# Five Strassen units instead of four in two output projections, woven in an order written out by hand

## The chip, the cores and the metric

The kernel runs on one core of a Trainium2 chip. The metric is the device time of one execution in microseconds (us); lower is better. TensorE is PE in the profile (its weight loads PEld), VectorE is DVE, ScalarE is ACT, GpSimd is POOL and SyncE is SP.

## The reference

The whole kernel computes two residual layers on 512 tokens of width 1024: a dilated attention mixer and an mLSTM mixer, each followed by a gated FFN of width 2816, and a last RMS norm. The change concerns only the second matrix product of the two FFNs, and the norm that follows the second:

```python
def swiglu(xn, w_in, w_out):
    gu = xn @ w_in
    return (jax.nn.silu(gu[..., :D_FF]) * gu[..., D_FF:]) @ w_out      # [512, 2816] @ [2816, 1024]

for i in range(2):
    ...
    h = h + swiglu(rms_norm(h, ffn_norm[i]), ffn_w_in[i], ffn_w_out[i])
return rms_norm(h, final_norm)
```

All of it is float32.

## The kernel before

**Split products.** Each float32 operand is split into a high part in TensorE's fp32r format and a low part, the difference. One product is made of three matmuls: high by high, high by low, low by high (`SPLITS`). Splitting a chunk of weights costs an ACT copy (`whi`, line 209) and a DVE subtract (`wlo`, line 210) of 128x1024 elements; splitting an operand of hidden rows costs an ACT copy (line 1114) and a DVE subtract (line 1108) of 128x512.

**The output projection.** The 2816 rows of `w_out` are eleven pairs of row tiles (a pair is 2 x 128 rows), the 1024 columns two halves, and the 512 tokens two halves. `output_products` (line 1090) does part of this by the Strassen-Winograd scheme of two by two by two blocks: a unit takes two row pairs, both column halves and both token halves, and does seven products P1, P2, P5, P6, P7, P3 and P4 in place of eight. The operands of these are sums and differences of weights and of hidden rows. `UNITS = 4` units cover eight row pairs; the three other pairs (`REST`) are done plainly, once for each column half, and are called plain or rest items. In layer 0 a product is 24 matmuls of 256 columns, a rest item 24 of 512 (`tile_mm`, line 1289, matmul at line 1292); in layer 1 a product is 12 matmuls of 512 columns, a rest item 24 (`multiply_half`, matmul at line 1674).

**Sums of weights.** In layer 1 each unit keeps a running sum `t` of weight chunks (tile f1T, 128x1024), which passes through P1, P5, P6 and P4: after P1 and after P5 it is negated on ACT (line 1163), and a DMA issued by POOL adds other weight rows from DRAM to it (`add_rows`, line 1160); after P6 it is negated again. P7 loads another chunk, to which DVE adds `t` (line 1182; line 1177 in layer 0), and then a DMA adds rows to `t` for P4. P2, P3, P7 and the rest items load raw chunks through SP (`load_chunk`, line 201) into a ring of `W_BUFS = 3` buffers. The high and low parts have rings of three too. So a raw load waits for the low split of the load three before it, and a high split waits for the matmuls of the item three before it. Layer 0 has sums of hidden rows instead, and for P5 a sum of two weight chunks that a load and an accumulating DMA make early (`load_first_sum`, line 1123).

**Order.** The items stand in a list: all P1, P5 and P2 in turns, all P6, P7 and the first column half's rest items in turns, all P3, P4 in turns with what is left of the second half's rest items, and at the end the last `tail` rest items (2 in layer 0, 3 in layer 1). `work` (line 1261) goes through the list and prepares the item two places ahead before it issues the matmuls of an item. The tail's items are done tile by tile: one output tile after the other gets the products of all of them, so that the first tile's output can go on while the others are computed. Preparations are issued in the order that the scheduler gives, and each engine's queue runs in that order: an instruction that waits holds up those behind it.

```python
PR = lambda name: [("product", name, u) for u in range(UNITS)]
items = (PR("P1") + merge(PR("P5"), PR("P2")) + PR("P6") + merge(PR("P7"), rest[first]) + PR("P3")
         + merge(PR("P4"), rest[second][:-tail]) + last)
```

**What follows.** In layer 0 `first_tiles` adds the first column half to the residual after the last P3 (`natural`, tile hn, line 1309) and the rest after the tail; the next norm (tiles n2ssum, n2sq, n2_h and n2_l) starts from these. In layer 1 `outputs` and `output` add the residual (tile ht) and square it on ACT (fsq); the tail's loop ends with the final norm for each of four token tiles: root on ACT, reciprocal and two small steps on DVE, a scaling on ACT (line 1744) and one on DVE (line 1746), and the stores. The gains `gbc` of the final norm are one tile of 1024 columns, which a DMA fills and POOL multiplies by -0.5.

The names of weight tiles carry layer, product, unit and part: f1P_2w_h is the high part of the weights of some product for unit 2 in layer 1 (the profile leaves out the product's number), and f1w_h that of a rest item.

Of the kernel before, what the change touches and what calls it, by code (L numbers as in the profile page):

```python
# [71 lines left out]
def tile_hybrid_dilated_attn_mlstm(  # L72
# [1017 lines left out]
    def output_products(layer, fp, wo, sums_of_rows, tail):  # L1090
# [6 lines left out]
        UNITS = 4  # L1097
        REST = range(2 * UNITS, FC // 2)
        hid, ops, whl, sums, tw = [], {}, {}, [], []
# [10 lines left out]
        def split_operand(name, u, src):  # L1110

            t = fp.tile([P, 2, 2, HALF], F32R, tag="op%d" % (UNITS * (PARTS.index(name) % 3) + u),
                        name="f%d%s_%d" % (layer, name, u))
            nc.scalar.activation(t[:, 0], src, AF.Copy)  # L1114
            subtract(t[:, 1], src, t[:, 0].bitcast(F32))
            ops[name, u] = [[t[:, part, k] for k in range(2)] for part in range(2)]
# [6 lines left out]
        def load_first_sum(u):  # L1123

            src = [weight_rows(hk * UNITS + u, 1) for hk in range(2)]
            if u == 0:
                t = fp.tile([P, 2, 512], F32, tag="t1", name="f%dS1_0" % layer)
                parts = [(t, slice(0, 2))]
            else:
                tags = ((), (("u2", 1), ("v5", 1)), (("gu1", 2),) * 2, (("gu0", 3),) * 2)[u]  # L1130
                parts = [(fp.tile([P, 1, 512], F32, tag=tg, name="f%dS1_%d" % (layer, u), bufs=bufs), slice(k, k + 1))
                         for k, (tg, bufs) in enumerate(tags)]
# [18 lines left out]
        def prepare_product(name, u):  # L1151
            nm = "f%d%s_%dw" % (layer, name, u)
            view = lambda t: t.rearrange("p (k n) -> p k n", k=2)

            def load(hk, n):
                return load_chunk(weight_rows(hk * UNITS + u, n), [P, 2, 512], nm)[0]

            def add_rows(to, hk, n):

                nc.gpsimd.dma_start(view(to), weight_rows(hk * UNITS + u, n), accum_op=ALU.add)  # L1160

            def negate(x):
                nc.scalar.activation(x, x, AF.Copy, scale=-1.0)
            if name == "P1":
                if u % 2 == 0:
                    tw.append(fp.tile([P, 2, 1024], F32, tag="w8", name="f%dT%d" % (layer, u), bufs=2))
                nc.sync.dma_start(view(tw[u // 2][:, u % 2]), weight_rows(u, 0))
            t = tw[u // 2][:, u % 2]
            in_place = ("P1", "P6", "P3") if sums_of_rows else ("P1", "P5", "P6", "P4")
            if sums_of_rows and name == "P5":  # L1170
                prepare_first_sum(u, t, nm)
                return
            raw = t if name in in_place else load(*ROWS[name])
            if sums_of_rows:

                if name == "P7":
                    nc.vector.tensor_tensor(raw, raw, t, op=ALU.add)
                    add_rows(t, 1, 0)


            elif name == "P7":
                nc.vector.tensor_tensor(raw, raw, t, op=ALU.add)
                add_rows(t, 1, 0)
            whl[name, u] = split_chunk((raw, 1024, view, nm))
            if sums_of_rows and name == "P1":

                for i in {0: (0,), UNITS - 1: range(1, UNITS)}.get(u, ()):
                    load_first_sum(i)
            if sums_of_rows:
                if name == "P6":  # L1190
                    negate(t)
            elif name in ("P1", "P5"):
                negate(t)
                add_rows(t, int(name == "P5"), 1)
            elif name == "P6":
                negate(t)

            if name == "P2":
                if ("P2", u) not in ops:
                    split_operand(name, u, half(UNITS + u, 0))  # L1200
            elif name == "P5":
                split_operand(name, u, sums[u])
            elif name == "P6":
                split_operand(name, u, half(u, 1))
            elif name == "P7":
                subtract(sums[u], half(u, 1), half(u, 0) if sums_of_rows else half(UNITS + u, 1))
                split_operand(name, u, sums[u])
            elif name == "P3":
                if not sums_of_rows:
                    subtract(half(u, 1), half(UNITS + u, 0), half(u, 1))  # L1210
                split_operand(name, u, half(UNITS + u, 1) if sums_of_rows else half(u, 1))
            elif name == "P4":
                if sums_of_rows:
                    subtract(half(UNITS + u, 0), half(UNITS + u, 0), half(u, 1))
                split_operand(name, u, half(UNITS + u, 0 if sums_of_rows else 1))

        def prepare_rest(n, pi):
            if pi not in ops:
                i = pi - REST[0]

                hi = (fp.tile([P, 2, SEQ], F32R, tag="op%d" % (3 * UNITS + i), name="f%dhh%d" % (layer, pi)) if i < 2 else
                      xp.tile([P, 2, SEQ], F32R, tag="x%d" % (pi - 4), name="f%dhh%d" % (layer, pi)))
                nc.scalar.activation(hi, hid[pi], AF.Copy)
                tags = (("u2", 1), ("v5", 1)) if i == 0 else (("gu%d" % (2 - i), 1 + i),) * 2
                lo = [fp.tile([P, SEQ], F32R, tag=tg, name="f%dhl%d" % (layer, pi), bufs=bufs) for tg, bufs in tags]
                for k in range(2):
                    subtract(lo[k], hid[pi][:, k], hi[:, k].bitcast(F32))
                ops[pi] = [hi[:, k] for k in range(2)], lo
            whl[n, pi] = split_chunk(load_chunk(weight_rows(pi, n), [P, 2, 512], "f%dw%d_%d" % (layer, n, pi)))

        def during(j, i):
            u = j // 2 - (FC // 2 - UNITS)
            if i == 1 and 0 <= u < UNITS:
                sums.append(fp.tile([P, 2, HALF], F32, tag="sums", name="f%dS%d" % (layer, u), bufs=UNITS))
# [6 lines left out]
            if j == FC - 2 and 3 <= i:  # L1241
# [4 lines left out]
        PR = lambda name: [("product", name, u) for u in range(UNITS)]  # L1246
# [14 lines left out]
        def work(product, plain, then):  # L1261

            for i, (kind, *key) in enumerate(items[:-tail]):
# [8 lines left out]
            for i in range(len(items) - tail + AHEAD, len(items)):  # L1272
                prepare(i)
            return [(ops[pi], whl[n, pi]) for _, n, pi in last]
# [3 lines left out]
    with ExitStack() as fctx:  # L1278
        fp = pool(fctx, "ffn0")
        hid, during, prepare, work = output_products(0, fp, ffn_w_out[0], True, 2)  # L1280
# [41 lines left out]
        def first_tiles():  # L1322
            for m in range(4):
                natural(m, F[0][m])
        last = work(product, plain, {("P1", 3): lambda: copy_half(0), ("P5", 3): lambda: copy_half(1),
                                     ("P6", 3): lambda: add_sum(0), ("P7", 3): lambda: add_sum(1),
                                     ("P3", 3): first_tiles})
        for m in range(4):
            for b, w in last:
                tile_mm(F[1][m], m, b, w)  # L1330
# [299 lines left out]
    with ExitStack() as fctx:  # L1630
# [3 lines left out]
        TAIL = 3  # L1634
        hid, operands, prepare, work = output_products(1, fp, ffn_w_out[1], False, TAIL)
# [42 lines left out]
        def output(tb, n, acc, part, cs=slice(0, 512)):  # L1678
# [4 lines left out]
            if n == 0:  # L1683
                nc.gpsimd.tensor_tensor(t, t, gbc[:, cs], op=ALU.mult)
# [29 lines left out]
        last = work(product, plain, {("P1", 3): lambda: copy_banks(u_, c11), ("P5", 3): lambda: copy_banks(c22, p5),  # L1714
                                     ("P6", 3): lambda: add_banks((0, 1), u_), ("P7", 3): lambda: add_banks((2, 3), u_),
                                     ("P4", 0): lambda: outputs((0, 1), p5), ("P4", 1): lambda: outputs((2, 3), c22)})
# [6 lines left out]
        for acc, tb, cs in tiles:  # L1723
            for i, (a, w) in enumerate(last):
                for k in range(2):
                    for a_, b_ in SPLITS:
                        nc.tensor.matmul(acc[:, cs], a[a_][k][:, tb * P:(tb + 1) * P], w[b_][:, k, cs],
                                         start=(acc is rest_of and i == 0 and k == 0 and (a_, b_) == SPLITS[0]),
                                         stop=(i == TAIL - 1 and k == 1 and (a_, b_) == SPLITS[-1]),
# [4 lines left out]
            else:  # L1734
# [11 lines left out]
                nc.vector.scalar_tensor_tensor(t1, t1, r, gbc[:, 512:], op0=ALU.mult, op1=ALU.mult)  # L1746
# [25 lines left out]
```

## Time and profile before

| | |
|---|---|
| median of 3 runs | 1408.92 us (1408.32 to 1408.97) |
| profiled execution | 1409.1 us, span 1407.0 us |
| TensorE | busy for 99% of the span |
| DVE, ACT, POOL | 74%, 47%, 10% |
| layer 0's output projection | 731.6 to 845.3 us of the span |
| layer 1's output projection and the end | 1291 to 1407 us of the span |

The span is that of the profiled execution on the chip, from its first to its last instruction; the 2.1 us between it and the time lie around it. Lines of the page and of the trace's views are shown in the prediction. A row of a group has engine, line, operation, tile written and tiles read, the count, and then the durations and the first and last starts; a row of a timeline has start, duration, engine, line, operation, and in brackets how long the engine stood idle before and what released it.

### The profile page before, as it was taken

What the parts mean: (1) busy time and instruction counts of PE and PEld (TensorE: products, weight loads), DVE (VectorE), ACT (ScalarE), POOL (GpSimd) and SP (SyncE); (2) the same over time, 40 slices, a digit from 0 to 9 for tenths busy, and PEclk for the clock granted to TensorE, in tenths of its full rate; (3) what the DMA queues carried; (4) which work ended last, traced back from release to release, by engine and by line L of the source; (5) the groups of instructions that cost most, each with busy time, mean ns of one, the idle gap of its engine ahead of it and who ended that gap; (6) DMA issues with size and microseconds to landing.
All of it is one profiled execution on the core that took longest, in us unless ns stands there. A gap on an engine that the chain in (4) does not pass through costs nothing.

```text
span 1407.0 us, 21031 instructions
## 1 busy us (share of the span) xinstructions
PE 1395.9 (99%) x8154; PEld 1235.5 (88%) x8154; DVE 1045.6 (74%) x1816; ACT 659.5 (47%) x1096; POOL 145.4 (10%) x216
## 2 busy tenths in 40 slices
PE   9999999999999999999999999999999999999998
PEld 7888888888888888999999998888888899999886
DVE  7866557566567298777877788998758888887785
ACT  5333224224225153444576354786534444458744
POOL 1011011002002000000010101113101230002111
PEclk9999999999999999999999999999999999999999
DMA  6346245334434444333264543234333553335871
GB/s 194 98 113 201 77 117 154 125 105 129 163 102 120 160 118 152 91 120 118 67 186 97 150 120 84 85 90 103 96 101 105 168 151 116 120 99 141 173 188 61
DMA packets 136381, 174.44 MB, mean 124 GB/s; under 512 B 8469, under 2 KB 111189, under 8 KB 136281
## 3 DMA queue, kind: packets, MB, share of 16 engines
q1 hardware_dynamic: 121088, 133.65, 30.3%
q0 software_dynamic: 13536, 38.33, 12.3%
q8 instruction: 64, 1.05, 0.3%
q10 hardware_dynamic: 1656, 1.12, 0.2%
q14 instruction: 37, 0.30, 0.1%
HBM read 157.34 MB, written 15.73 MB: 123 GB/s over the span
## 4 chain that ended last, share of the span: by engine, by line
PE 92%; DVE 5%; ACT 2%; issue 1%; ACTq 0%; DVEq 0%
PE fo L1292 8%; PE f0j_u L1017 5%; PE f1j_u L1017 5%; PE f1j L240 5%; PE f0j L240 5%; PE f1j_p L1017 3%; PE f0j_p L1017 3%; PE f1j_c L1017 3%; PE f0j_c L1017 3%; PE mwo L240 3%; PE awo L240 3%; PE mo L240 3%; PE finu L1674 2%; PE finc L1674 2%; PE finp L1674 2%; PE a3g12v L298 2%
## 5 line engine op out<-in xcount | busy, mean ns | idle before, releaser
L240 PE MATMUL f0j<-n_h,f0j_h 128*128 128x512 f32 x96 | 37.5, 390 | 0.0
L240 PE MATMUL f1j<-n_h,f1j_h 128*128 128x512 f32 x96 | 37.5, 390 | 0.0
L240 PE MATMUL f1j<-n_h,f1j_l 128*128 128x512 f32 x96 | 37.4, 389 | 0.0
L240 PE MATMUL f0j<-n_h,f0j_l 128*128 128x512 f32 x96 | 37.4, 389 | 0.0
L240 PE MATMUL f0j<-n_l,f0j_h 128*128 128x512 f32 x96 | 37.3, 389 | 0.0
L240 PE MATMUL f1j<-n_l,f1j_h 128*128 128x512 f32 x96 | 37.3, 389 | 0.0
L1135 POOL DMA_DIRECT2D f0S<-in_ffn_w_out_dram x7 | 6.5, 1019 | 265.6 <-ACT f0P L1114 146.6
L1644 POOL DMA_DIRECT2D hD<-hB x32 | 20.7, 653 | 96.3 <-DVE hB L1641 96.3
L539 DVE TENSOR_TENSOR rot<-rot,sinr 32x1024 f32<-32x1024 f32 x24 | 28.9, 1205 | 0.0
L240 PE MATMUL mo<-n_h,mo_k_h 128*128 128x512 f32 x64 | 25.3, 395 | 0.0
L240 PE MATMUL mo<-n_h,mo_k_l 128*128 128x512 f32 x64 | 25.2, 394 | 0.0
L240 PE MATMUL mo<-n_l,mo_k_h 128*128 128x512 f32 x64 | 25.1, 393 | 0.0
L240 PE MATMUL mqk<-n_h,mqk_k_h 128*128 128x512 f32 x64 | 25.1, 393 | 0.0
L240 PE MATMUL mwo<-yo_l,mwo_k_h 128*128 128x512 f32 x64 | 25.1, 393 | 0.0
L240 PE MATMUL mqk<-n_l,mqk_k_h 128*128 128x512 f32 x64 | 25.1, 392 | 0.0
L240 PE MATMUL awo<-ao_h,awo_k_h 128*128 128x512 f32 x64 | 25.1, 392 | 0.0
L240 PE MATMUL mwo<-yo_h,mwo_k_l 128*128 128x512 f32 x64 | 25.0, 391 | 0.0
L240 PE MATMUL mqk<-n_h,mqk_k_l 128*128 128x512 f32 x64 | 25.0, 390 | 0.0
L240 PE MATMUL awo<-ao_h,awo_k_l 128*128 128x512 f32 x64 | 25.0, 390 | 0.0
L240 PE MATMUL awo<-ao_l,awo_k_h 128*128 128x512 f32 x64 | 24.9, 390 | 0.0
L240 PE MATMUL mwo<-yo_h,mwo_k_h 128*128 128x512 f32 x64 | 24.9, 391 | 0.0
L240 PEld LDWEIGHTS f0j<-n_h,f0j_l 128*128 128x128 f32 x96 | 18.0, 188 | 3.8
(2271 smaller groups left out, 5427.9 us busy)
## 6 DMA issues: line engine op xcount, KB each, us to landing
f0j_w<-in_ffn_w_in_dram SPq DMA_DIRECT2D x28, 512.0 KB, 4.4
f1j_w<-in_ffn_w_in_dram SPq DMA_DIRECT2D x28, 512.0 KB, 4.1
f1T<-in_ffn_w_out_dram POOLq DMA_DIRECT2D x12, 512.0 KB, 7.0
awo_k_w<-in_attn_w_out_dram SPq DMA_DIRECT2D x8, 512.0 KB, 5.8
mv_k_w<-in_mlstm_w_in_dram SPq DMA_DIRECT2D x8, 512.0 KB, 3.7
mqk_k_w<-in_mlstm_w_in_dram SPq DMA_DIRECT2D x8, 512.0 KB, 3.8
mo_k_w<-in_mlstm_w_in_dram SPq DMA_DIRECT2D x8, 512.0 KB, 3.7
mwo_k_w<-in_mlstm_w_out_dram SPq DMA_DIRECT2D x8, 512.0 KB, 3.5
```

The costliest lines, as they stand in the source:

```text
L240: nc.tensor.matmul(acc, whl[a][:, k, m * P:(m + 1) * P], pairs[b][kk], start=(kk == 0 and (a, b) == SPLITS[0]), stop=(kk == nk - 1 and (a, ...
L298: nc.tensor.matmul(accs[tb], pairs[a][kk][:, tb * P:(tb + 1) * P], whl[b][:, k, :], start=(kk == 0 and (a, b) == SPLITS[0]), stop=(kk == K ...
L539: nc.vector.tensor_tensor(sh, sh, sinr.unsqueeze(1).to_broadcast([R, 2, SEQ]), op=ALU.mult)
L1017: nc.tensor.matmul(acc[name][:, m * HALF:(m + 1) * HALF], whl[a][:, k, m * P:(m + 1) * P], ops[okey][b][:, k], start=(fresh and m == 0 and ...
L1135: nc.gpsimd.dma_start(t, src[1][:, ks], accum_op=ALU.add)
L1292: nc.tensor.matmul(acc, w[a_][:, k, m * P:(m + 1) * P], b[b_][k], start=(fresh and k == 0 and (a_, b_) == SPLITS[0]), stop=(k == 1 and (a_ ...
L1644: nc.gpsimd.dma_start(hD[k // 4].rearrange("(b i) x -> i b x", i=R)[:, :, c0:c0 + R], t[R * a_:R * (a_ + 1)])
L1674: nc.tensor.matmul(acc[m], a[a_][k][:, (2 * t + m) * P:(2 * t + m + 1) * P], w[b_][:, k, :], start=(fresh and k == 0 and (a_, b_) == SPLIT ...
```

## The change

`UNITS` becomes 5 in both layers, so that ten row pairs go through the seven products and one pair is left: two rest items, one for each column half. The order of the items is written out, the same for both layers. It takes up P6 of a unit while P5 and P2 of later units run, and P3 and P4 of the first units while P7 and P3 of later ones run. The tail is three items in both layers: P4 of units 3 and 4 and the last rest item. In layer 0 the two products of the tail have half the columns; in layer 1 they touch token tiles 2 and 3 alone, and tiles 0 and 1 need the rest item only.

The difference of hidden rows that P7 needs is made at P6. The fifth unit's tiles go to buffers that other parts of the kernel have left: its running sum to the tag t1, its late operands to gu0, its sum of hidden rows to the norm's ssum; the early weight sums of layer 0 and the rest pair's operands change their buffers too. The final gains become two tiles of 512 columns, loaded in `load_gains` after the last P7 item's matmuls are issued.

```diff
-    def output_products(layer, fp, wo, sums_of_rows, tail):
-        UNITS = 4
+    def output_products(layer, fp, wo, sums_of_rows):
+        UNITS = 5
+        TAIL = 3
         REST = range(2 * UNITS, FC // 2)
...
         def split_operand(name, u, src):
-            t = fp.tile([P, 2, 2, HALF], F32R, tag="op%d" % (UNITS * (PARTS.index(name) % 3) + u),
-                        name="f%d%s_%d" % (layer, name, u))
-            nc.scalar.activation(t[:, 0], src, AF.Copy)
-            subtract(t[:, 1], src, t[:, 0].bitcast(F32))
+            i = UNITS * (PARTS.index(name) % 3) + u
+            nm = "f%d%s_%d" % (layer, name, u)
+            if i < 2 * len(PRODUCTS):
+                t = fp.tile([P, 2, 2, HALF], F32R, tag="op%d" % i, name=nm)
+                hi, lo = t[:, 0], t[:, 1]
+            else:
+                hi, lo = [fp.tile([P, 2, HALF], F32R, tag="gu0", name=nm, bufs=3) for _ in range(2)]
+            nc.scalar.activation(hi, src, AF.Copy)
+            subtract(lo, src, hi.bitcast(F32))
...
             if name == "P1":
-                if u % 2 == 0:
-                    tw.append(fp.tile([P, 2, 1024], F32, tag="w8", name="f%dT%d" % (layer, u), bufs=2))
-                nc.sync.dma_start(view(tw[u // 2][:, u % 2]), weight_rows(u, 0))
-            t = tw[u // 2][:, u % 2]
+                if u < 4:
+                    if u % 2 == 0:
+                        w8.append(fp.tile([P, 2, 1024], F32, tag="w8", name="f%dT%d" % (layer, u), bufs=2))
+                    tw.append(w8[-1][:, u % 2])
+                else:
+                    tw.append(fp.tile([P, 1024], F32, tag="t1", name="f%dT%d" % (layer, u)))
+                nc.sync.dma_start(view(tw[u]), weight_rows(u, 0))
+            t = tw[u]
...
-                for i in {0: (0,), UNITS - 1: range(1, UNITS)}.get(u, ()):
+                for i in {0: (0,), 1: (1,), UNITS - 1: range(2, UNITS)}.get(u, ()):
                     load_first_sum(i)
...
             elif name == "P6":
                 split_operand(name, u, half(u, 1))
+                subtract(sums[u], half(u, 1), half(u, 0) if sums_of_rows else half(UNITS + u, 1))
             elif name == "P7":
-                subtract(sums[u], half(u, 1), half(u, 0) if sums_of_rows else half(UNITS + u, 1))
                 split_operand(name, u, sums[u])
...
-        rest = {n: [("rest", n, pi) for pi in REST] for n in range(2)}
-        last = rest[second][-tail:]
-        merge = lambda *lists: [e for group in itertools.zip_longest(*lists) for e in group if e]
-        items = (PR("P1") + merge(PR("P5"), PR("P2")) + PR("P6") + merge(PR("P7"), rest[first]) + PR("P3")
-                 + merge(PR("P4"), rest[second][:-tail]) + last)
+        order = ("P1_0 P1_1 P1_2 P1_3 P1_4 P5_0 P2_0 P5_1 P2_1 P6_0 P5_2 P2_2 P6_1 P5_3 P2_3 P6_2 P5_4 P2_4 P6_3 P6_4 "
+                 "P7_0 first P7_1 P7_2 P3_0 P7_3 P3_1 P7_4 P3_2 P3_3 P4_0 P3_4 P4_1 P4_2 P4_3 P4_4 second").split()
+        items = [("rest", first if e == "first" else second, REST[0]) if "_" not in e else ("product", e[:2], int(e[3:]))
+                 for e in order]
...
         for m in range(4):
-            for b, w in last:
-                tile_mm(F[1][m], m, b, w)
+            for kind, b, w in last:
+                tile_mm(F[1][m][:, ts[0]] if kind == "product" else F[1][m], m, b, w)
             natural(4 + m, F[1][m])
...
-        gbc = fp.tile([P, D], F32, tag="t1", name="gbc")
-        nc.gpsimd.dma_start(gbc, final_norm.unsqueeze(0).to_broadcast([P, D]))
-        nc.gpsimd.tensor_scalar(gbc, gbc, -0.5, None, op0=ALU.mult)
+        def load_gains():
+            for n, tag in enumerate(("rbc", "ssum")):
+                gbc.append(npl.tile([P, 512], F32, tag=tag, name="gbc"))
+                nc.gpsimd.dma_start(gbc[n], final_norm[n * 512:(n + 1) * 512].unsqueeze(0).to_broadcast([P, 512]))
+                nc.gpsimd.tensor_scalar(gbc[n], gbc[n], -0.5, None, op0=ALU.mult)
+        def after_p7():
+            add_banks((2, 3), u_)
+            load_gains()
...
         for acc, tb, cs in tiles:
-            for i, (a, w) in enumerate(last):
+            todo = [e for e in last if tb >= 2 or e[0] == "rest"]
+            for i, (kind, a, w) in enumerate(todo):
+                block = tb - 2 if kind == "product" else tb
...
```

More of the change, by code (lines that the diff above doesn't have):

```diff
@@ L1218, in prepare_rest @@
             if pi not in ops:
[L1219 to L1225, printed above, removed]
+                two = lambda name, *tags: [fp.tile([P, SEQ], F32R, tag=tg, name="f%dh%s%d" % (layer, name, pi), bufs=bufs)
+                                           for tg, bufs in tags]
+                hi, lo = two("h", ("gu1", 2), ("gu1", 2)), two("l", ("u2", 1), ("v5", 1))
                 for k in range(2):
-                    subtract(lo[k], hid[pi][:, k], hi[:, k].bitcast(F32))
-                ops[pi] = [hi[:, k] for k in range(2)], lo
+                    nc.scalar.activation(hi[k], hid[pi][:, k], AF.Copy)
+                    subtract(lo[k], hid[pi][:, k], hi[k].bitcast(F32))
+                ops[pi] = hi, lo
             whl[n, pi] = split_chunk(load_chunk(weight_rows(pi, n), [P, 2, 512], "f%dw%d_%d" % (layer, n, pi)))
@@ L1261, in work @@
         def work(product, plain, then):
-            for i, (kind, *key) in enumerate(items[:-tail]):
+            for i, (kind, *key) in enumerate(items[:-TAIL]):
                 prepare(i + AHEAD)
@@ L1271, in work @@
                     plain(*key, ops[key[1]], whl[key])
-            for i in range(len(items) - tail + AHEAD, len(items)):
+            for i in range(len(items) - TAIL + AHEAD, len(items)):
                 prepare(i)
-            return [(ops[pi], whl[n, pi]) for _, n, pi in last]
+            return [(kind, ops[(a, b) if kind == "product" else b], whl[a, b]) for kind, a, b in items[-TAIL:]]
         return hid, during, prepare, work
@@ L1683, in output @@
             if n == 0:
-                nc.gpsimd.tensor_tensor(t, t, gbc[:, cs], op=ALU.mult)
+                nc.gpsimd.tensor_tensor(t, t, gbc[0][:, cs], op=ALU.mult)
         def mean_before(tb):
```

55 lines of the change are left out of this document (28 added, 27 removed).

## The prediction

> **What bounds the kernel now.** I read the page's busy times and chain first, then the busy time by stretches (columns: length of the stretch; busy us and count of PE, PEld, DVE, ACT, POOL; granted clock; DMA share; GB/s) for the two places that the change touches, then the groups of single tiles, the engines' timelines and the DMA issues.
> ```profile
> span 1407.0 us, 21031 instructions
> ...
> PE 1395.9 (99%) x8154; PEld 1235.5 (88%) x8154; DVE 1045.6 (74%) x1816; ACT 659.5 (47%) x1096; POOL 145.4 (10%) x216
> ...
> PE 92%; DVE 5%; ACT 2%; issue 1%; ACTq 0%; DVEq 0%
> ```
> ```profile
> core 0: us, PE busy (x) PEld busy (x) DVE busy (x) ACT busy (x) POOL busy (x), PEclk, DMA share, GB/s
> 731.60:845.30 113.70, 113.70 (x820) 107.97 (x819) 89.03 (x113) 60.96 (x81) 8.47 (x13) 1.00 0.49 128
> 1291.00:1386.00 95.00, 95.00 (x421) 78.47 (x420) 71.96 (x90) 60.28 (x75) 13.24 (x11) 1.00 0.67 150
> ```
> PE is busy for the whole of both output projections (113.70 of 113.70, 95.00 of 95.00), at the full granted clock. So matmuls removed count fully, and so does every microsecond for which PE finds its operands unready. DVE stands at 78% and 76% there, and layer 1 keeps the DMA engines at 0.67: DVE's order and the DMAs are what can become late. The profiled execution took 1409.1 us with a span of 1407.0; the median of the runs is 1408.92, so I add the sum to 1409.1 and take 0.2 off.
>
> **PE's saving.** The first and last starts of equal tiles of four units give the pace.
> ```profile
> L1292 PE MATMUL fo<-f0P,f0P_0w_h x112: 283/283/283, 731.7 to 819.9; 128*128 128x256 f32 x112
> ...
> L1292 PE MATMUL fo<-f0P,f0P_3w_h x112: 277/283/283, 740.4 to 834.0; 128*128 128x256 f32 x112
> ```
> ```profile
> L1674 PE MATMUL finu<-f1P_0w_h,f1P x24: 389/389/500, 1323.6 to 1375.2; 128*128 128x512 f32 x24
> ...
> L1674 PE MATMUL finu<-f1P_3w_h,f1P x24: 389/389/389, 1331.8 to 1383.4; 128*128 128x512 f32 x24
> ```
> Three products of layer 0 take 740.4-731.7: 2.90 us each (24 matmuls of 256 columns, 0.121 apart). Three of layer 1 take 1331.8-1323.6: 2.73 each (12 of 512 columns, 0.228 apart), and a plain item, 24 of 512 columns, takes twice that, 5.46. Each layer loses four plain items (21.8) and gains seven products: 20.3 in layer 0, 19.1 in layer 1. Saved: 1.5 + 2.7 = 4.2. The counts are fixed in the built order of PE (layer 0: 672 matmuls of 256 and 144 of 512 columns become 840 and 48), so that the saving isn't made at all has no chance worth a figure. The Trainium skill, "TensorE: Matmul & The Clock Gate", section "Back-to-back issue gap", gives an isolated gap of N/2.4 + 2.5 ns, 109 ns for 256 columns where the trace has 121; by it the saving would be about 5.0 and the forecast 0.8 lower. I keep the trace.
>
> **Layer 0's tail.** From the first tile of P3_4 on, DVE's order is hn0, P4_2's lo weights, hn1 to hn3, P4_3's lo weights, one subtract of hidden rows, n2ssum, n2_l, P4_3's lo operand, P4_4's lo weights, subtract, n2ssum, n2_l, P4_4's lo operand. The durations, start to start:
> ```profile
> 815.28 1.12 DVE L1309 TENSOR_TENSOR hn<-fo,h 128x512 f32<-128x512 f32 x1 [1.35 <-PE fo L1292]
> 816.23 1.21 DVE L210 TENSOR_TENSOR f0w_l<-f0w_w,f0w_h 128x1024 fp32r<-128x1024 f32 x1
> 817.37 3.50 DVE L1309 TENSOR_TENSOR hn<-fo,h 128x512 f32<-128x512 f32 x3
> 820.70 1.22 DVE L210 TENSOR_TENSOR f0P_1w_l<-f0P_1w_w,f0P_1w_h 128x1024 fp32r<-128x1024 f32 x1
> 821.83 0.68 DVE L1108 TENSOR_TENSOR f0hid<-f0hid,f0hid 128x512 f32<-128x512 f32 x1
> 822.43 1.48 DVE L838 TENSOR_TENSOR n2ssum<-n2ssum,n2sq 128x512 f32<-128x512 f32 x2
> 823.82 0.69 DVE L1108 TENSOR_TENSOR f0P<-f0hid,f0P 128x512 fp32r<-128x512 f32 x1
> 824.43 1.22 DVE L210 TENSOR_TENSOR f0P_2w_l<-f0P_2w_w,f0P_2w_h 128x1024 fp32r<-128x1024 f32 x1
> ...
> 828.16 0.75 DVE L228 SCALAR_TENSOR_TENSOR n_l<-hn,cols,n_h 128x512 fp32r<-128x512 f32 x1
> ```
> The first five steps take 821.83-815.28 = 6.55; then 0.60, 0.70 and 0.75 (n_l), P4_3's operand 0.61, and 1.13 + 0.60 + 0.70 + 0.75 + 0.69: 13.1 in all, begun 0.7 after P3_4's start, so ready at 13.8 less some 0.2 of overlaps. PE has P3_4, P4_1, P4_2 and all of P4_3 before it: 4 x 2.90 = 11.6. Stall 2.0. In before, plain items stand between the P4s and cover the same list. Ends: 0 if PE is late by then anyway; 3.6 if P4_4's hi operand, behind two more ACT operations, comes 1.6 later.
>
> **Layer 1.** Only three raw weight buffers turn round: a load may start when the lo split of three loads earlier is done. Prices of splits, sums and landings (the last: min, median and max of all accumulating DMAs):
> ```profile
> 1332.00 1.06 ACT L209 ACTIVATE f1w_h<-f1w_w 128x1024 fp32r<-128x1024 f32 x1 [0.19 <-PE finu L1674]
> 1332.96 0.61 ACT L1114 ACTIVATE f1P<-f1hid 128x512 fp32r<-128x512 f32 x1
> ```
> ```profile
> 1335.43 1.22 DVE L1182 TENSOR_TENSOR f1P_1w_w<-f1P_1w_w,f1T 128x1024 f32<-128x1024 f32 x1
> ```
> ```profile
> f1w_w<-in_ffn_w_out_dram SPq DMA_DIRECT2D x4, 512.0 KB, 3.9
> f1T<-in_ffn_w_out_dram POOLq DMA_DIRECT2D x3, 512.0 KB, 6.7
> f1P_2w_w<-in_ffn_w_out_dram SPq DMA_DIRECT2D x2, 512.0 KB, 4.2
> f1P_3w_w<-in_ffn_w_out_dram SPq DMA_DIRECT2D x2, 512.0 KB, 4.4
> f1P_0w_w<-in_ffn_w_out_dram SPq DMA_DIRECT2D x1, 512.0 KB, 7.5
> ```
> ```profile
> f1w_w<-in_ffn_w_out_dram SPq DMA_DIRECT2D x1, 512.0 KB, 5.9
> ```
> ```profile
> DMA to landing us min/median/max: 6.0/7.0/9.5
> ```
> (a) DVE has P7_0's add ahead of P5_3's lo split, and P7_0's load starts after P2_2's lo. Landing L, add 1.14 (1.22 busy, start to start as above) and split 1.22 stand against P2_2 and P6_1, 5.46 of PE. How early P2_2's lo is, before does not show: I take half a product, 1.4. With L near 5.1 (between 4.4 and 5.9): 0.6; ends 0 (L 3.9) and 3.0 (L 7.5).
> (b) P6_4's weights come from P5_4's by an accumulating DMA, only three items later: negation 1.06, landing 6.7, hi 1.06, lo 1.22 against three products, 8.2: 1.8; ends 0 (P5_4's lo early by as much) and 4.6 (landing 9.5).
> (c) After P6_4's lo, ACT negates (1.06), copies P7_4's operand (0.61) and only then splits the first plain item's weights (1.06, then lo 1.22), of which PE's order wants two matmuls right after P6_4: 3.95 against 2.73: 1.2; ends 0 and 1.2.
> (d) DVE holds P7_1's, P3_0's and P3_1's lo splits behind the adds of P7_2, P7_3 and P7_4, and each of those loads waits for the lo split before. Counted from the plain item's lo, with P7_2's load issued 1.2 earlier, P3_1's lo is ready at L1+L2+L3 + 3 x (1.14+1.22) - 1.2 = L1+L2+L3 + 5.9; PE comes to it after P7_0 (2.73), 22 plain matmuls (5.0), four products (10.9) and two single matmuls: 19.1. The stall is L1+L2+L3 - 13.2. P7_2's load runs before the accumulates: 4.4; P7_3's and P7_4's beside them and beside P3's loads: 7.5 and 5.9. Stall 4.6; ends 0 (three of 3.9) and 9.3 (three of 7.5). In before, the plain items' 5.46 stand between the P7s, and the P3s follow with no adds between.
> (e) The last plain item's weights can be split only after P4_2's matmuls, behind a square of about 0.6 on ACT: 0.6 + 1.06 + 1.22 against ten matmuls (2.3): 0.6; ends 0 and 1.1 (one more square).
>
> **The end.** Tile 2's reciprocal, two steps and scaling now stand on DVE behind the add of the last matmuls, ahead of tile 3's. The same operations of tile 3:
> ```profile
> 1401.39 0.16 DVE L1737 SCALAR_TENSOR_TENSOR fv<-fss,fpre 128x1 f32<-128x1 f32 x1 [0.57 <-ACT fsq L1682]
> 1401.81 0.16 DVE L1740 RECIPROCAL fr<-fr 128x1 f32<-128x1 f32 x1 [0.27 <-ACT fr L1739]
> 1402.01 0.27 DVE L1741 TENSOR_SCALAR fa<-fr,fv 128x1 f32<-128x1 f32 x1
> 1402.32 0.16 DVE L1742 SCALAR_TENSOR_TENSOR fr<-fa,fr 128x1 f32<-128x1 f32 x1
> 1402.52 0.75 DVE L1746 SCALAR_TENSOR_TENSOR ht<-ht,fr,gbc 128x512 f32<-128x512 f32 x1
> ```
> 0.16+0.27+0.16+0.75 = 1.3, of which the idle 0.57 ahead of fv takes some; ACT scales tile 2 too ahead of tile 3's root. I take 1.0; ends 0 and 1.8.
>
> **At nothing:** the P7 sums made at P6 (0.6 each on DVE, in its 22%), the places of the first sums and of the fifth unit (other buffers, free by then), and the gains in halves: on POOL the second half's DMA waits ahead of P7_4's accumulate, which only P4_4, eight items later, needs; without that cover it is one landing, 6.7.
>
> **The sum:** 2.0+0.6+1.8+1.2+4.6+0.6+1.0 = 11.8, less 4.2: +7.6. Profiled 1416.7, on the runs' median **1416.5**. All low ends give 1404.7, all high ends 1429. No cost goes below nothing, since PE has no idle time in these stretches to give back.
>
> **Rivals.** (B) PE stays the bound, as it is now with DVE at 78%: every split keeps ahead, and only the end costs 1.0. -3.2: 1405.7, faster. It decides if L1+L2+L3 stays under 13.2 and P4_4's operand comes within 11.6 of P3_4; the DVE list speaks against it, the 3.9 row for it. (C) Transfers land at their shortest, loads at 3.9 and accumulates at 6.0: (a) and (d) go, (b) is 1.1, the fixed orders stay: 5.9 - 4.2 = +1.7, 1410.6, no change that can be told. For it speak the 3.9 to 4.4 rows; against it the DMA share of 0.67. The Trainium skill, "DMA: Bandwidth & Descriptors", section "Anatomy of one DMA — SWDGE (gpsimd) path", fits 2.0 us plus bytes over 436 GB/s, 3.2 for 512 KB; by it (b) goes too and the time is 1409.5. The accumulates' 6.0 at the least disagree. (D) DMA saturates, every load 7.5 and accumulate 9.5: (a) 3.0, (b) 4.6, (d) 9.3, with the rest 21.7 - 4.2 = +17.5: 1426.4. One row each speaks for it.
>
> **How the numbers follow.** My forecast's case has 0.60, B 0.15, C 0.18, D 0.07. Faster by over 0.2% (2.8 us, about what a measurement of this kernel can tell from no change) is B: 0.15; within it C: 0.18; slower the rest: 0.67. The range 1405.5 to 1421.5 leaves out D, the upper part of the forecast's case (all of (d) at its high end) and a little of B's low side, 0.2 together.
>
> **What would show it.** After's timeline should have PE idle before P4_4 in layer 0 (released by DVE's operand), before P6_4 (by the accumulate), before the first plain item's lo, and most at P3_0 and P3_1, where DVE waits in an add for a load; PE's last matmul should end 6.6 later, and the end after it take a microsecond longer. PE fully busy in both stretches, with the last matmul 4 earlier, would prove me wrong.

## The result, and the profile after

| | before | after |
|---|---|---|
| median | 1408.95 us (6 runs) | 1420.46 us (6 runs, 1419.72 to 1421.78) |
| profiled execution | 1409.1, span 1407.0 | 1421.78, span 1420.0 |

The change makes the kernel slower: after over before is 1.0083, 95% interval 1.0070 to 1.0095, or 11.5 us. The forecast was 1416.5 with a range to 1421.5: the sign was right, the size 4 us short.

The page of after, its span, busy times and chain:

```profile
span 1420.0 us, 21262 instructions
...
PE 1397.8 (98%) x8214; PEld 1237.7 (87%) x8214; DVE 1064.7 (75%) x1843; ACT 672.1 (47%) x1120; POOL 152.3 (11%) x225
...
PE 23%; DVE 5%; issue 5%; DMA 2%; ACT 2%; POOL 1%; POOLq 0%; ACTq 0%; DVEq 0%
```

The shares of this chain add up to 38%: it can be followed back only to about 865 us, so its 23% for PE cannot be set against the 92% of before (l0_five, below, takes no longer than before, and its page has 32% for PE). What is new is that DMA and POOL stand in it, with 2% and 1%; they stand in no chain of before or l0_five. Where the time goes the busy times by stretches show (layer 0's projection, layer 1's, the end; columns as in the prediction):

```profile
core 0: us, PE busy (x) PEld busy (x) DVE busy (x) ACT busy (x) POOL busy (x), PEclk, DMA share, GB/s
732.80:846.20 113.40, 112.50 (x890) 109.88 (x889) 95.61 (x124) 66.74 (x92) 10.28 (x10) 1.00 0.50 126
1292.00:1411.20 119.20, 111.98 (x488) 90.47 (x486) 86.02 (x114) 72.47 (x98) 23.36 (x19) 0.97 0.61 133
1411.20:1420.00 8.80, 0.00 (x0) 0.00 (x0) 4.38 (x14) 2.76 (x8) 1.43 (x2) 0.73 0.53 204
```

From the first and last starts of the output tiles' matmuls (fo; finc to finlast) I take three lengths for each kernel: layer 0, 113.2 before and 113.4 after; layer 1, 109.1 and 118.9; from the last matmul's start to the end of the span, 7.0 and 9.1. So layer 0 gives 0.2, layer 1 9.9 and the end 2.1. The profiled execution of after was the slowest of its six, 1.3 above their median. It also reached layer 0 1.1 later, in code that is the same; between the other profiles below that start varies from 731.3 to 732.6, so I give it no cause.

PE's timeline of after has these idle times in the two stretches, and no others. The number in brackets is the idle time, behind the arrow what ended it. The rows without brackets show delays that are not counted as idle time:

```profile
833.20 0.28 PE L1301 MATMUL fo<-f0P,f0P_2w_l 128*128 128x256 f32 x1
833.56 0.39 PE L1301 MATMUL fo<-f0P,f0P_3w_h 128*128 128x256 f32 x1
834.76 0.39 PE L1301 MATMUL fo<-f0P,f0P_3w_h 128*128 128x256 f32 x1 [0.82 <-DVE f0P L1109]
...
838.10 0.66 PE L1301 MATMUL fo<-f0P,f0P_4w_h 128*128 128x256 f32 x2
838.59 0.28 PE L1301 MATMUL fo<-f0P,f0P_4w_l 128*128 128x256 f32 x1
...
1328.14 0.50 PE L1690 MATMUL finp<-f1P_3w_l,f1P 128*128 128x512 f32 x1 [0.30 <-DVE f1P_3w_l L210]
...
1345.88 0.49 PE L1690 MATMUL finu<-f1P_4w_h,f1P 128*128 128x512 f32 x1 [1.35 <-ACT f1P_4w_h L209]
...
1347.13 0.79 PE L1690 MATMUL finu<-f1P_4w_l,f1P 128*128 128x512 f32 x1 [0.76 <-DVE f1P_4w_l L210]
...
1366.90 0.50 PE L1690 MATMUL finp<-f1P_0w_l,f1P 128*128 128x512 f32 x1 [1.59 <-DVE f1P_0w_l L210]
...
1373.64 0.50 PE L1690 MATMUL finp<-f1P_1w_l,f1P 128*128 128x512 f32 x1 [1.00 <-DVE f1P_1w_l L210]
...
1383.31 0.49 PE L1690 MATMUL finp<-f1P_3w_h,f1P 128*128 128x512 f32 x1 [1.45 <-ACT f1P_3w_h L209]
...
1384.57 0.80 PE L1690 MATMUL finp<-f1P_3w_l,f1P 128*128 128x512 f32 x1 [0.77 <-DVE f1P_3w_l L210]
```

In order: P4_3 in layer 0, and P4_4 without brackets; then in layer 1 P5_3, P6_4 (high, then low weights), P3_0, P3_1 and P3_3 (high, then low). The waits of layer 1 add up to 7.2. What stands behind them, from the timelines of ACT and DVE:

```profile
1344.77 1.06 ACT L209 ACTIVATE f1P_4w_h<-f1T 128x1024 fp32r<-128x1024 f32 x1 [2.17 <-DMA f1T<-in_ffn_w_out_dram]
```
```profile
1364.49 1.23 DVE L1189 TENSOR_TENSOR f1P_3w_w<-f1P_3w_w,f1T 128x1024 f32<-128x1024 f32 x1 [4.56 <-DMA f1P_3w_w<-in_ffn_w_out_dram]
1365.63 1.22 DVE L210 TENSOR_TENSOR f1P_0w_l<-f1P_0w_w,f1P_0w_h 128x1024 fp32r<-128x1024 f32 x1
```
```profile
1382.21 1.06 ACT L209 ACTIVATE f1P_3w_h<-f1P_3w_w 128x1024 fp32r<-128x1024 f32 x1 [5.01 <-DMA f1P_3w_w<-in_ffn_w_out_dram]
```
and the loads from the timeline of SP's queue:
```profile
1356.22 0.37 SPq L201 DMA_DIRECT2D f1P_3w_w<-in_ffn_w_out_dram  x1
...
1373.62 0.37 SPq L201 DMA_DIRECT2D f1P_3w_w<-in_ffn_w_out_dram  x1
```
P6_4's high split waits for the accumulating DMA. DVE stands 4.56 us in P7_3's add, waiting for a load that took 8.3 (1356.22 to 1364.49), with P3_0's low split queued right behind. P3_3's load took 8.6 (1373.62 to 1382.21).

A second loss is not a wait. After two of these places the granted clock (the column behind the counts of POOL) is at half:

```profile
1346.00:1348.00 2.00, 1.24 (x3) 0.83 (x4) 2.00 (x2) 1.66 (x2) 0.00 (x0) 0.76 0.00 0
1348.00:1350.00 2.00, 2.00 (x6) 1.51 (x6) 0.55 (x2) 2.00 (x4) 0.00 (x0) 0.50 0.28 48
1350.00:1352.00 2.00, 2.00 (x10) 1.60 (x9) 2.00 (x3) 0.66 (x2) 0.00 (x0) 0.88 0.71 229
1384.00:1386.00 2.00, 1.43 (x3) 1.17 (x4) 2.00 (x4) 1.16 (x2) 0.00 (x0) 0.65 0.00 0
1386.00:1388.00 2.00, 2.00 (x6) 1.61 (x5) 2.00 (x4) 0.00 (x0) 0.00 (x0) 0.50 0.03 8
```
(0.24+0.50+0.12) x 2 = 1.7 us of full clock are missing at P6_4 and (0.35+0.50) x 2 = 1.7 at P3_3. Layer 1 then adds up: -2.7 saved, +7.2 waits, +3.4 clock, and 2.0 left for seven waits, about 0.3 each: the time from start to start is longer than the idle time shows, and the matmul behind a wait is recorded at about 0.50 where the others have 0.39. This is the sum of one execution; what the half clock really cost is taken up below.

### The profile page after: what moved, and what is told of

It is laid out like the page before. It is cut to its first block, busy times and chain, and to the rows that moved or that the text cites. A ratio compares the mean times of both kernels' runs of the same rounds, so it can differ in the third digit from the quotient of the medians.

```text
span 1420.0 us, 21262 instructions
## 1 busy us (share of the span) xinstructions
PE 1397.8 (98%) x8214; PEld 1237.7 (87%) x8214; DVE 1064.7 (75%) x1843; ACT 672.1 (47%) x1120; POOL 152.3 (11%) x225
## 3 DMA queue, kind: packets, MB, share of 16 engines
q8 instruction: 64, 1.05, 0.3%
## 5 line engine op out<-in xcount | busy, mean ns | idle before, releaser
L1163 POOL DMA_DIRECT2D f1T<-in_ffn_w_out_dram x15 | 18.2, 1211 | 192.8 <-DMA f1P_2w_w<-in_ffn_w_out_dram 131.2
```

## The experiments

Each stands beside runs of before on the same chip; before's medians there are 1408.97 to 1409.08. "Layer 1", "end", "waits" and "clock" are read as above (the clock from its mean in stretches of 10 us between 1290 and 1400).

| run | median us | ratio to before, 95% | layer 1 | end | waits of PE | clock lost |
|---|---|---|---|---|---|---|
| before | 1408.95 | | 109.1 | 7.0 | 0 | 0 |
| after | 1420.46 | 1.0070 to 1.0095 | 118.9 | 9.1 | 7.2 | 3.4 |
| l0_five | 1409.29 | 0.9993 to 1.0012 | 109.1 | 7.4 | 0 | 0 |
| l1_five | 1420.23 | 1.0069 to 1.0099 | 118.5 | 8.8 | 7.5 | 1.7 |
| filler | 1423.20 | 1.0081 to 1.0114 | 119.8 | 9.1 | 5.1 | 1.7 |
| ring | 1415.78 | 1.0032 to 1.0062 | 113.2 | 9.1 | 3.6 | 1.7 |
| plain_before_p64 | 1410.25 | 1.0003 to 1.0021 | 107.5 | 9.0 | 0.7 | 0 |
| grouped | 1411.78 | 1.0010 to 1.0029 | 109.7 | 9.1 | 1.5 | 0 |
| tail_rows | 1419.65 | 1.0060 to 1.0090 | 119.7 | 7.4 | 9.5 | 0 |
| three_edits | 1409.22 | 0.9991 to 1.0011 | 110.1 | 7.3 | 2.5 | 0 |
| woven_again | 1411.26 | 1.0009 to 1.0027 | 109.9 | 8.8 | 1.7 | 0 |
| two_tails | 1410.36 | 1.0003 to 1.0020 | 107.5 | 8.8 | 1.1 | 0 |
| woven_layer0 | 1418.82 | 1.0060 to 1.0085 | 110.5 | 8.8 | 2.0 | 0 |
| plain_earlier | 1408.42 | 0.9988 to 1.0005 | 110.3 | 7.1 | 2.7 | 0 |

The last four columns are those of one profiled execution. It took 1421.78 in after, 1411.0 in three_edits and 1410.41 in plain_earlier, above their medians, and 1408.71 in plain_before_p64 and 1408.99 in two_tails, below theirs.

### One layer at a time

In each, the other layer keeps before's code.

```diff
-        hid, during, prepare, work = output_products(0, ...)
+        hid, during, prepare, work = output_products4(0, ...)      # l1_five: layer 0 as before
```

> Five units in layer 0 only; layer 1 as before. Theory (the fixed order of DVE and ACT costs a stall at the tail that eats the saved matmuls): layer 0's stretch is within 0.5 us of before and the time within 0.6 us of before, about 1409. Rival (the products saved count in full in layer 0): 1407.4. Second rival (layer 0 carries part of the loss): over 1410.5.

> Five units in layer 1 only; layer 0 as before. Theory (all of the loss is in layer 1 and the end): 1420, PE idle at the same places as in the changed kernel. Rival (part of the loss came through layer 0 or through something that the two layers share): under 1418.

1409.29 and 1420.23: layer 0 costs nothing and gains nothing, and the whole loss is layer 1's with the end behind it. So the 1.5 us of matmuls saved in layer 0 are used up there, and after's rows above show where. At 0.12 from start to start P4_3's second matmul would have started at 833.44, behind P4_2's last at 833.20; it started at 834.76, 1.3 late (0.82 of it counted as idle). At P4_4 two matmuls take 0.49 (838.10 to 838.59) in place of 0.24, another 0.25. Together that is 1.6.

### The clock

```diff
         def product(name, u, a, w):
             multiply_half(target[name], a, 0, w, ...)
+            if (name, u) in (("P6", 3), ("P3", 2)):
+                for _ in range(9):
+                    nc.tensor.matmul(target[name][1], zero, w[0][:, 0, :], start=False, stop=False, ...)
```

> The changed kernel, with nine matmuls of 512 columns with a zero operand after P6_3 and nine after P3_2 in layer 1, which add zero to the same banks in the time in which PE stands idle before P6_4 and P3_3. Theory (a wait of this length costs twice: the wait itself, and then some 3.4 us at half the granted clock, 1.7 us each): the clock stays full there, and the time falls by 2.5 to 3.5 us, to about 1417.3. Rival (the half clock does not hang on PE standing idle): no fall; the fillers are hidden or add up to 1 us: 1420 to 1421.5.

A miss: 1423.20, slower than after and above the rival's range too. PE's waits and the clock by stretches in filler:

```profile
1347.32 0.50 PE L1690 MATMUL finu<-f1P_4w_l,f1P 128*128 128x512 f32 x1 [0.18 <-DVE f1P_4w_l L210]
...
1367.88 0.50 PE L1690 MATMUL finp<-f1P_0w_l,f1P 128*128 128x512 f32 x1 [1.97 <-DVE f1P_0w_l L210]
...
1392.22 0.50 PE L1690 MATMUL finp<-f1P_4w_l,f1P 128*128 128x512 f32 x1 [1.33 <-DVE f1P_4w_l L210]
```
```profile
1360.00:1370.00 10.00, 8.03 (x35) 6.26 (x34) 5.08 (x6) 3.05 (x4) 1.20 (x1) 0.96 0.70 168
1370.00:1380.00 10.00, 10.00 (x40) 8.18 (x39) 8.41 (x11) 4.03 (x5) 4.93 (x3) 0.87 1.03 252
```

At the two filled places the clock stayed full. But nothing was won: PE waited 1.97 at P3_0 in place of 1.59, now with the half clock behind that, and a wait of 1.33 appeared at P3_4. The eighteen matmuls put in take 4.1 us themselves (0.228 each), and how much of that lay outside the waits this run does not tell. tail_rows (below) is the cleaner comparison: its order up to P4_1 is that of after, and its clock was full throughout.

```profile
1345.70 0.51 PE L1692 MATMUL finu<-f1P_4w_h,f1P 128*128 128x512 f32 x1 [1.27 <-ACT f1P_4w_h L209]
...
1384.15 0.51 PE L1692 MATMUL finp<-f1P_3w_l,f1P 128*128 128x512 f32 x1 [0.76 <-DVE f1P_3w_l L210]
```

It comes to P3_3's low weights 93.0 us after layer 1's start (1384.15 - 1291.17), after itself in 92.6 (1384.57 - 1291.97), though after had lost 1.7 of clock on the way. From P6_4 to P3_3 the preparations set the pace; a slow PE is only a shorter wait at the next place, and the theory that a wait costs twice falls for this stretch.

Behind P3_3 no wait follows in after, and there the second half clock did cost time. l1_five shows how much, for its layer 1 is that of after and its clock was full from P3_3 on:

```profile
1383.71 0.50 PE L1877 MATMUL finp<-f1P_3w_l,f1P 128*128 128x512 f32 x1 [0.76 <-DVE f1P_3w_l L210]
...
1397.22 0.39 PE L1877 MATMUL finu<-f1P_2w_h,f1P 128*128 128x512 f32 x1
...
1399.41 0.73 PE L1933 MATMUL finc<-f1w_h,f1hh 128*128 128x512 f32 x2 [0.45 <-ACT f1w_h L209]
...
1409.32 0.28 PE L1933 MATMUL finlast<-f1w_h,f1hl 128*128 128x256 f32 x1
```

From P3_3's low weights to P4_2's last matmul l1_five takes 13.5 (1383.71 to 1397.22) and after 14.9 (1384.57 to 1399.45): 1.4 more. To PE's last matmul it is 25.6 and 26.4 (to 1410.92), only 0.7 more, because l1_five then waits at the last plain item and after, being later, does not. So even there about half of the lost clock came back as a wait less.

### The ring of raw buffers

```diff
+            if layer == 1 and (name, u) == ("P7", 3):
+                parts = [fp.tile([P, SEQ], F32, tag="gu0", ...) for _ in range(2)]     # not in the ring
+                ... load, add, split these two halves
             raw = t if name in in_place else load(*ROWS[name])
```

> The changed kernel, with P7_3's raw weights in layer 1 in two free tiles outside the ring of three raw buffers, so that its load needs no lo split of P7_1, and P7_4's load needs P7_2's lo split in place of P3_0's. Theory (loads start late because of the ring): the waits at P3_0 (1.6), P3_1 (1.0) and P3_3 (1.5 + 0.8) go, and the half clock behind the last (1.7): 1413 to 1415. Rival (the DMA engines are full from 1360 to 1382 us and loads land late wherever they start): P3_0's wait is moved, the sum of the waits falls by less than 2: 1418.5 to 1420.5.

1415.78, 4.7 below after, a microsecond short of the expectation but on its side. The waits at P3_0, P3_1 and P3_3 are gone; these two are all that is left behind P5_3:

```profile
1347.32 0.50 PE L1706 MATMUL finu<-f1P_4w_h,f1P 128*128 128x512 f32 x1 [2.05 <-ACT f1P_4w_h L209]
1348.58 0.67 PE L1706 MATMUL finu<-f1P_4w_l,f1P 128*128 128x512 f32 x1 [0.76 <-DVE f1P_4w_l L210]
```
And the DMA engines, in the same profile, are as full as ever without PE waiting for them:
```profile
1360.00:1370.00 10.00, 10.00 (x46) 8.28 (x45) 8.45 (x13) 5.06 (x7) 1.81 (x2) 1.00 1.07 260
1370.00:1380.00 10.00, 10.00 (x45) 8.27 (x45) 8.45 (x12) 4.90 (x6) 1.38 (x3) 1.00 0.93 253
```
So the long landings hurt because each load had to wait for a split that stood behind an add that waited for the load before. Full DMA engines alone do not make the loss.

### The plain item ahead of P6_4

```diff
-    ... P6_3 P6_4 P7_0 first P7_1 ...
+    ... P6_3 first P6_4 P7_0 P7_1 ...            # on top of ring
```

> The run 'ring' with the first plain item moved ahead of P6_4 in layer 1, so that P5_4's accumulating DMA has two items more (5.46 us) before P6_4 needs its result. Theory (the wait before P6_4 is the chain negation, DMA, splits, and three items are too few for it): that wait (2.05 + 0.76) and the half clock behind it (1.7) go, against 1415.8 of 'ring': 1411 to 1412. Rival (PE's waits only move to the next late preparation, as in 'filler'): waits appear at the P7s or P3s instead, 1414 to 1416.

1410.25, 5.5 below ring. In the profiled execution, the fastest of ten, one wait is left in layer 1, and it is a new and small one:

```profile
1351.17 0.47 PE L1708 MATMUL finu<-f1P_0w_h,f1P 128*128 128x512 f32 x1 [0.67 <-ACT f1P L1120]
```
Layer 1 takes 107.5 there, 1.6 less than before: here the saved matmuls show. The end still takes 9.0. The ten executions spread from 1408.71 to 1414.05, before's on that chip from 1408.36 to 1409.73; what the slower ones lost no trace shows.

### The old grouping for five units

```diff
+    if layer == 1:                 # P1s; P5 and P2 in turns; P6s; P7_0 first P7_1 to P7_4; P3s; P4s; second
+        order = (...)
```

> The changed kernel, with layer 1's items in groups as before had them, for five units: P1s, P5 and P2 in turns, P6s, P7s with the first plain item after P7_0, P3s, P4s, last plain item; the tail stays P4_3, P4_4 and the last plain item. Theory (the hand-written order makes the waits, not the fifth unit): P6_4 is five items after P5_4, and no add stands between the P3s, so the waits before P6_4, P3_0, P3_1 and P3_3 go: 1410 to 1413, with PE waiting only where five P7s follow each other. Rival (five units leave too few plain items to cover the preparations, in any order): 1417 or more.

1411.78, as expected in the time. One of the waits that were to go is still there: at P3_1, which is now two items behind the last P7, PE stands idle for 0.50 and 0.76. Five units in the old grouping cost 2.7 us over before, most of it at the end (9.1 against 7.0); the hand-written order in layer 1 costs 8.7 more. So 8.7 of the 11.5 us come from the order, not from the fifth unit.

### The end

```diff
-    ... P4_0 P3_4 P4_1 P4_2 | P4_3 P4_4 second      # | : what follows is done tile by tile
+    ... P4_0 P3_4 P4_1 second | P4_2 P4_3 P4_4      # layer 1 only
```

> The changed kernel, with the last plain item of layer 1 taken out of the tail and put between P4_1 and P4_2, the tail being P4_2 to P4_4, so that tiles 0 and 1 of the last norm are finished while P4s run. (Layer 0 gets the same order string as in the changed kernel.) Theory (the end is 2 us longer because the norms of three tiles fall together after the last matmuls): the time between PE's last matmul and the end goes from 8.8 back to about 6.7, 1418 to 1418.7 in all. Rival (the end is set by the stores and by the last tile alone): 1420 to 1421.

1419.65: the end went from 9.1 to 7.4, as expected, but only half of that reached the time, since P4_4's splits came late (waits of 0.25 and 1.14). What the end of after consists of, DVE's timeline from the last matmuls on:

```profile
1408.78 2.42 DVE L1765 SCALAR_TENSOR_TENSOR ht<-ht,fr,gbc 128x512 f32<-128x512 f32 x2
1411.12 0.15 DVE L1756 SCALAR_TENSOR_TENSOR fv<-fss,fpre 128x1 f32<-128x1 f32 x1
...
1413.02 1.18 DVE L1765 SCALAR_TENSOR_TENSOR ht<-ht,fr,gbc 128x512 f32<-128x512 f32 x1
1414.12 0.15 DVE L1756 SCALAR_TENSOR_TENSOR fv<-fss,fpre 128x1 f32<-128x1 f32 x1
```
Tile 3's own step (fv at 1414.12) starts 2.9 after PE's last matmul ended (1411.2), where before it was 1.1 (1400.3 to 1401.39). In between stand tile 2's steps, from its fv at 1411.12 on. They come so late because DVE scales tiles 0 and 1 ahead of them; the two scalings take 2.42. Tile 2's scaling then takes 1.18 where before's took 0.75. The group of the four scalings of after, before's scaling of tile 2, and what ACT and POOL do in after meanwhile:

```profile
L1765 DVE SCALAR_TENSOR_TENSOR ht<-ht,fr,gbc x4: 740/966/1758, 1408.8 to 1415.2; 128x512 f32<-128x512 f32 x4
```
```profile
1398.92 0.75 DVE L1746 SCALAR_TENSOR_TENSOR ht<-ht,fr,gbc 128x512 f32<-128x512 f32 x1
```
```profile
1406.41 1.28 ACT L1758 ACT_TABLE_LOAD   x1
1407.70 0.29 ACT L1758 ACTIVATE fr<-fv 128x1 f32<-128x1 f32 x2
```
```profile
1408.69 1.30 POOL L1700 TENSOR_TENSOR ht<-ht,gbc 128x512 f32<-128x512 f32 x1 [0.75 <-ACT fsq L1698]
...
1412.22 1.43 POOL L1700 TENSOR_TENSOR ht<-ht,gbc 128x256 f32<-128x256 f32 x2 [2.24 <-ACT fsq L1698]
```
The roots of tiles 0 and 1 start behind ACT's load of a table, 1.28 us. Before has its load for this step at 1389.36, 10.7 us ahead of its last matmul, and tail_rows at 1401.25, 9.6 ahead; in after it is 4.5. So three things came together late in after: tiles 0 and 1, the table and tile 2. tail_rows moves the first two, and no run separates them.

### Together, and further

Layer 1's order in these runs, from P6_3 on, all with the ring's edit:

```diff
-    P6_3 P6_4 P7_0 first P7_1 P7_2 P3_0 P7_3 P3_1 P7_4 P3_2 P3_3 P4_0 P3_4 P4_1 P4_2 | P4_3 P4_4 second            # after
+    P6_3 first P6_4 P7_0 P7_1 P7_2 P3_0 P7_3 P3_1 P7_4 P3_2 P3_3 P4_0 P3_4 P4_1 second | P4_2 P4_3 P4_4            # three_edits
+    P6_3 first P6_4 P7_0 P7_1 P7_2 P3_0 P7_3 P3_1 P7_4 P3_2 P3_3 P4_0 P3_4 P4_1 second P4_2 | P4_3 P4_4            # two_tails
+    P6_3 first P6_4 P3_0 P7_0 P7_1 P3_1 P7_2 P3_2 P7_3 P7_4 P3_3 P4_0 P3_4 P4_1 second P4_2 | P4_3 P4_4            # woven_again
+    P6_3 first P6_4 P7_0 P7_1 P7_2 P3_0 P7_3 P3_1 P7_4 P3_2 P3_3 P4_0 P3_4 second P4_1 | P4_2 P4_3 P4_4            # plain_earlier
```

> Three edits together: P7_3's weights outside the ring, the first plain item ahead of P6_4, the last plain item between P4_1 and P4_2, in layer 1. Theory (each removes its own loss): 1409 to 1410.5, within 0.1% of before; PE's waits in layer 1 add up to less than 1.5 us. Rival (waits move on): 1413 or more.

1409.22, as expected, though with 2.5 of waits where less than 1.5 was expected: of the loss nothing is left, and nothing is gained over before. Four runs tried for more.

> Three edits once more, with two other places in layer 1: P3_0 stands between P6_4 and P7_0, and the P3s go among the P7s one earlier, so that DVE's two adds for P6's banks lie beside P3_0; and the tail of layer 1 is only P4_3 and P4_4. Theory (where no wait is left, the 2.7 us of matmuls saved in layer 1 show): 1406.3, between 1405.5 and 1407.5, with waits of PE in layer 1 under 0.7 in all. Rival (DVE, with an add, a lo split, an operand and a sum for each P7, is the bound there and PE waits at some P7): 1408.5 or more.

> As woven_again, but with P7 and P3 in the changed kernel's order (no P3_0 before P7_0), which leaves P7_0 to wait for DVE's adds to P6's banks (1.3 in three_edits): it tells the new place of P3_0 from the shorter tail. Theory: 1407.6, 1.3 above woven_again. Rival (the tail alone makes the difference): equal to woven_again.

In woven_again the rival held: 1411.26, with PE waiting 0.77 and 0.76 for the low splits of P7_1 and P7_4. two_tails met neither its theory (1.3 slower than woven_again) nor its rival (equal): 1410.36, 0.9 faster; in its profiled execution, the fastest, it has only the wait before P7_0 (1.05). Their runs overlap (1408.99 to 1412.79 and 1410.78 to 1412.33), so P3_0 ahead of P7_0 gains nothing, and that it costs something is not shown.

```diff
+    if layer == 0:
+        order = "... P3_3 P4_0 P3_4 P4_1 second | P4_2 P4_3 P4_4"       # woven_layer0: woven_again, and this
```

> As woven_again, and in layer 0 too the last plain item stands between P4_1 and P4_2, so that 5.46 us more of matmuls lie beside DVE's list ahead of P4_3's operand. Theory (layer 0's wait of 0.8 to 1.1 at the tail goes, and nothing else is late): 1 us below woven_again, about 1405.3. Rival (the shorter tail leaves the next norm's preparation uncovered at the end of layer 0): equal to woven_again or slower.

A clear miss, on the rival's side: 7.6 slower than woven_again. The wait at P4_3 did not go either (0.37 and 0.70 are left). Layer 0 itself took 113.2, as in before; the loss stands behind it: from layer 0's last output matmul to layer 1's first it is 452.8, and 445.8 in woven_again. PE's timeline and the first stretch after layer 0 in woven_layer0:

```profile
850.28 1.84 PE L845 MATMUL n2ss<-ones,n2ssum 128*128 128x1 f32 x8 [3.47 <-DVE n2ssum L838]
```
```profile
845.00:860.00 15.00, 10.50 (x39) 8.37 (x38) 12.71 (x38) 5.16 (x9) 3.61 (x13) 0.77 0.28 74
```
The tail's plain item, 1.4 us for each output tile, was the cover of the next norm's squares and sums. Without it PE waits 3.5 for these, and 1.0 more at two other places of this stretch. The clock lacks 3.5 (0.23 x 15), part of it while PE stood idle; what it adds to the waits is at most the rest of the 7.0, about 2.5 us.

> As three_edits, with the last plain item of layer 1 one item earlier, between P3_4 and P4_1, so that P4_4's splits (0.6 of wait in three_edits) find DVE and ACT less full at the tail; the tail stays P4_2 to P4_4. Theory (PE's saving in layer 1, as in plain_before_p64, and the shorter end of tail_rows add up): 1408.3, 1.9 under plain_before_p64 and 0.7 under before. Rival (the tail's splits stay late, wherever the plain item stands): 1409.2 or more, as three_edits.

1408.42, ratio 0.9988 to 1.0005: the lowest median of all kernels here, and no difference from before that these runs can tell. The number is the theory's, but its mechanism is not shown: the wait for P4_4's low weights, which was to shrink, is 1.04 in the profiled execution (1410.41), and 0.56 in that of three_edits.

## Why the prediction was right in sign and short in size

- PE's saving, 4.2: the matmuls are gone, as the lengths of plain_before_p64 and two_tails show (layer 1 at 107.5 with waits of 0.7 and 1.1, against 109.1).
- Layer 0's tail, 2.0 at P4_4: DVE had P4_4's operand ready 13.6 after P3_4's start (824.68 to 838.32), as the sum has it. But most of the delay stood at P4_3, 1.3, and 0.25 at P4_4. The prediction's own list has P4_3's operand ready at 9.9, and PE comes to it after three products, 8.7; that wait was not drawn from it. The sum for layer 0 (+0.5) was near the measured +0.2.
- (a) 0.6 at P5_3: 0.30. (b) 1.8 at P6_4: 1.35 + 0.76, by the chain that was named; its accumulating DMA took 7.9 (issued at 1336.86, ACT starts at 1344.77) where 6.7 was taken. (c) 1.2 at the plain item: no wait in after, where PE had come late and slow from P6_4; in filler, with the clock full, it is there (0.30 + 0.76). (e) 0.6: none in after, 0.45 in l1_five, where the clock was full.
- (d), 4.6 by L1+L2+L3 - 13.2: 1.59 + 1.00. The loads landed in 3.9, 8.3 and 4.3 us, 16.5 in all, by which the formula gives 3.3. The mechanism held and ring removed it, and the formula is off by 0.7; the guesses for L2 (7.5) and L3 (5.9) were each off, in opposite directions.
- The step that failed is where (d) was ended: "the P3s follow with no adds between" was said of before, and for after I walked no further than P3_1. P3_3's load goes through the same ring behind P3_1's late split, and took 8.6: 1.45 + 0.77 of waits that stood at nothing.
- The clock had no term. It lost 3.4 in the profile; the first half of that, as tail_rows shows, stands in place of waits and not on top of them, and the second cost 0.7 at PE's last matmul, against l1_five.
- The end, 1.0 with an upper end of 1.8: 2.1. Tile 2's steps stood where they were expected; missing were the scalings of tiles 0 and 1 ahead of them (2.42), and that tile 2's scaling takes 1.18 in place of 0.75.

That the time still lies inside the range is in part luck. At the places of layer 1 that the sum prices it has 8.8, and the profile 5.0 (0.30 + 2.11 + 1.59 + 1.00). What it left out made up for that and more: 2.2 at P3_3, the delay from start to start behind each wait, the clock, and 1.1 more at the end. PE's last matmul ended 10.9 later than in before (1400.3 and 1411.2), where 6.6 was forecast.

Rival B (PE stays the bound) fails by the waits, C (transfers at their shortest) by landings of 8.3 and 8.6. D (saturated DMA) has the landings in part, but ring refutes it as the cause.

## What to carry to other kernels

An order written by hand has to be walked through every ring and every queue to its last item, not to the place where the new neighbours end: here nearly half of the waits of the load chain (2.2 of 4.8) stood two items behind the last add. When a preparation chain sets the pace, a gain on the engine that waits (a full clock, fewer matmuls) turns into longer waits; break the chain, by one buffer outside the ring and one longer item ahead of the late result, before counting matmuls. And an item that stands in a tail may be the cover of the next stage: look behind the stage's end before it is moved.

## What the runs showed of the hardware

- The granted clock fell to half for about 3.4 us (1.7 of clock lost) after waits of 1.35 and 0.76 with one matmul between them, and not after nearly the same waits in tail_rows (1.27 and 0.76); it fell after 1.97 alone in filler, and not after 1.94 in l1_five. The Trainium skill, "TensorE: Matmul & The Clock Gate", section "What's actually happening", has a free-running window of about 3.4 us, and the fall after an idle window. The length and the half agree; that an idle time of 2.1 in all is enough, in some runs and not in others, goes beyond it. A window whose position shifts would fit that; no run here shows the window itself.
- A scaling of 512 columns on DVE (line 1765) took 1.76 at 1408.78 and 1.18 at 1413.02, both begun while POOL multiplied tiles, and 0.74 and 0.75 for the two begun with POOL idle (min and max of the group's row; the 2.42 are the first two together). The overlap is from the timelines; no run took POOL's work away.
- Loads of 512 KB issued within 26 us of one execution (1348.24 to 1373.62) landed in 3.9 to 8.6 us.
